# Moving all preparation of the last product's weights to the feed-forward input, and two tiles without a running bank

## The chip, the core and the metric

The kernel runs on one core of a Trainium2 chip. The metric is the device time of one execution in microseconds: 1590.32 us is the median of three runs (1590.27 to 1590.42). Beside those runs one execution was recorded by the hardware profiler; its rows are what this document quotes. The engines of the core are TensorE (PE; its weight loads are PEld), VectorE (DVE), ScalarE (ACT), GpSimd (POOL) and SyncE (SP), which issues nearly all DMA transfers.

## The reference

One encoder layer is applied to two independent sequences of 512 tokens with 1024 channels, each with 256 memory tokens; everything is float32. What matters here:

```
h = rmsnorm(x) @ w_in                      # u, q, k, v, xq and three gates
branches = s5(u), diff_attention(q, k, v), cross_attention(xq, mem)
x = x + (sum of sigmoid(gate_n) * (branch_n @ w_up_n)) @ w_out
gate, up = split(rmsnorm(x) @ w_ffn_in)    # 1024 -> 2 x 2816
x = x + (silu(gate) * up) @ w_ffn_out      # 2816 -> 1024, "the last product"
y = rmsnorm(x)
```

Cross attention has four heads of width 128: per head and sequence, softmax(q k^T) over 256 memory tokens, times the memory values.

## The kernel before

**Number format.** A float32 product is made of three faster ones: each operand is split in a high and a low part (ScalarE casts the high part, VectorE subtracts it from the source to get the low part; `split`, L134 and L135, or with a scale L137 and L138), and TensorE adds high x high, high x low and low x high. A matmul moves 128 x 512 numbers; every matmul is issued from one helper, so all of them carry line 66.

**Planner and orders.** The program is written as a trace, and a planner orders each engine's instructions by simulated times before the kernel runs; on the chip every engine then works through its list in order. Three things bind the planner. `tc.issue_after(x)` puts the instructions of a block behind x on x's engine. `queued()` puts DMA transfers behind the last weight load on SyncE. Where `PE.on` is true, each TensorE instruction is pinned behind all those traced before it. `PE.on` is true in cross attention and differential attention, false in the feed-forward input up to its last tile, and true from that tile (21) on.

**Cross attention** (L567 to L731). 32 steps: four heads, two sequences, four blocks of 128 queries. Step i computes the scores of step i + 2 (three matmuls of 128 x 256, tile `sc`), the softmax on VectorE and ScalarE (`softmax_parts`: maximum, its scale, exponential, reciprocal, then a product, L541 to L550 and L701), transposes step i's probabilities (`tr`, two 128 x 128), splits them (`xpTh`, `xpTl`), and after each fourth step multiplies them with the values (six matmuls into `oo`). Between these parts `fill(n)` lets TensorE do other work from a queue (L684): the query projections of the later heads, two gates, the values and the first queries of differential attention. A unit of that queue is six matmuls of 512 columns (or as many columns in narrower ones). `fill` keeps an account: it adds n, and issues units while the account is over zero. `finish(g)` empties the queue until g is done; it is called before the scores of a new head. What is left at the end of the steps is done in a row (L727).

**The last product's weights.** The last product uses a scheme of seven products in place of eight over quadrants of the operands; for its weights, sums of quarters must be made and split. Of all the pieces (a piece is four 128 x 128 blocks), 28 are prepared ahead (`NPREP`) and kept in DRAM (`wD`): 16 with all seven parts, 12 with four of the seven. `prepare` (L457) is a generator that does half a piece at a time, or a whole small piece: it loads `raw` (two transfers, L443 and L445), splits three quarters into `hl` (L137 on ScalarE, L138 on VectorE) and writes them to `wD` (L472), makes four sums on GpSimd (L452 to L455), and splits and writes the four results. `raw` has four buffers, `hl` has one for three parts and two for four. `half_piece` advances the generator by one. The 16 full pieces are prepared in cross attention, one half at the end of each step, behind the exponential and the product that follows it; the 12 small ones in tiles 4 to 18 of the feed-forward input, one a tile, behind the tile's last tanh on ScalarE, its last sum on VectorE and its last weight sum on GpSimd.

**The feed-forward input** (L1177 to L1231). 22 tiles (KFF) of 128 gate and 128 up channels for both sequences, again with seven products of 12 matmuls each, 84 matmuls a tile. There are six PSUM banks (`mm`) and two more (`tr`). There are two ways through a tile:

- `running` (L1129, tiles 1 to 20): one bank collects four products, A11, S2, S3 and A22, one on top of the other. Between them ScalarE copies the bank's content (`kept_sum`, L1137: tiles p1, u2, u3), and the next product may be added only after that. VectorE makes four sums of other banks and copies (L1112); the bank's last content is read directly by VectorE (L1211).
- `products` and `quadrants` (tiles 0 and 21): each product has its own bank, ScalarE makes one copy (L1119), and VectorE makes seven sums (L1112). In tile 21 the seven products advance together over k, with the seventh in a `tr` bank.

`activate` multiplies with the norm's factors, applies the tanh (L1208) and writes the tile `ac`, which goes to DRAM (`aD`). The up half is multiplied on GpSimd (L1214), except where it lies in the running bank (L1211 on VectorE). `weights4` loads and splits a tile's weights and makes four sums of them on GpSimd (`ws`, L1032 to L1035). Before tile 20's `activate`, the weights of tile 21 are traced. With tile 21 the first operands of the last product are loaded (`act_pair`), summed and split (L980 to L983, `quad_split`). Then the last product begins, with seven banks at once.

Of the kernel before, what the change touches and what calls it, by code (L numbers as in the profile page):

```python
# [28 lines left out]
KFF = FF // P  # L29
# [10 lines left out]
NPREP = (16, 28)  # L40
# [32 lines left out]
def encoder(ctx: ExitStack, tc: tile.TileContext, a, out):  # L73
# [274 lines left out]
    with yielding(last_s):  # L348
        x_norm(0, norm[0], range(5, 8))
        _, bc = factor(ss1, DM)  # L350
# [106 lines left out]
    def prepare(es_, todo_):  # L457
        pq = es_.enter_context(tc.tile_pool(name="pq", bufs=1, side="right", reuse_waits="tile"))
        raws = []

        def load():
            if len(raws) < len(todo_):
                raws.append(pq.tile([P, 4, P], F32, tag="raw", name="raw", bufs=4))
                with queued():
                    raw_in(raws[-1], *todo_[len(raws) - 1][:2])

        def part(n_, j, w_):
            m, p, _ = todo_[n_]
            k = w_.shape[1]
            hl = pq.tile([P, k, 2, P], F32R, tag=f"hl{k}", name="hl", bufs=k // 2)  # L470
            split(hl[:, :, 0], hl[:, :, 1], w_, scale=0.5)
            nc.sync.dma_start(wD[m, p][:, j : j + k], hl.bitcast(F32))  # L472

        for _ in range(3):
            load()
        yield
        for n_, (m, p, k) in enumerate(todo_):
            load()
            if k == 7:
                part(n_, 4, raws[n_][:, 1:4])  # L480
            if k == 7 or n_ == 0:
                raw_sums(raws[n_])
                yield
            part(n_, 0, raws[n_])
            if n_ + 1 < len(todo_) and todo_[n_ + 1][2] == 4:
                raw_sums(raws[n_ + 1])
            yield
# [96 lines left out]
    xa = phase.enter_context(tc.tile_pool(name="xa", bufs=2, reuse_waits="tile"))  # L584
    xcol = phase.enter_context(tc.tile_pool(name="xcol", bufs=2, reuse_waits="tile"))

    pes = ExitStack()
    prep = prepare(pes, pieces[: NPREP[0]])
    next(prep)

    queue = []
    owed = 0

# [93 lines left out]
    for i in range(-AHEAD, len(steps) + 1):  # L689
        if i + AHEAD < len(steps):  # L690
            h, s, lt = steps[i + AHEAD]
            if h and s == lt == 0:
                finish(xq[h])
            ms = slice(s * NMEM, (s + 1) * NMEM)
            qh, ql = (q_[:, lt * P : (lt + 1) * P] for q_ in qs[h, s])
            sc = bank("sc")
            PE.matmul(sc[:, :NMEM], qh, mkh[h][:, ms], start=True, stop=False)
            PE.matmul(sc[:, :NMEM], qh, mkl[h][:, ms], start=False, stop=False)
            PE.matmul(sc[:, :NMEM], ql, mkh[h][:, ms], start=False, stop=True)
            e, r = softmax_parts(xa, xcol, sc[:, :NMEM], NMEM, P ** -0.5, "x", bufs=3)  # L700
            last_e = last_x, V.tensor_scalar_mul(e, e, r)  # L701
            es[i + AHEAD] = e
        fill(9 if i == 0 else 5)
        if 0 <= i < len(steps):
            h, s, lt = steps[i]
            if lt == 0:
                pT[h, s] = tuple(slot("xT", [P, 2, L], F32R, n_) for n_ in ("xpTh", "xpTl"))
            e = es.pop(i)
            tr = aux()
            for j in range(2):  # L710
                PE.transpose(tr[:, j * P : (j + 1) * P], e[:, j * P : (j + 1) * P], ident)
            split(*(p_[:, :, lt * P : (lt + 1) * P] for p_ in pT[h, s]), tr[:, : 2 * P].rearrange("p (j q) -> p j q", j=2))
        fill(5 if i < len(steps) else 15)
        if i > 0 and steps[i - 1][2] == 3:
            h, s, _ = steps[i - 1]
            pTh, pTl = pT.pop((h, s))
            oo = bank("oo")
            hs = slice(h * P, (h + 1) * P)
            for j in range(2):
                PE.matmul(oo, mvh[s][:, j, hs], pTh[:, j, :], start=(j == 0), stop=False)  # L720
                PE.matmul(oo, mvh[s][:, j, hs], pTl[:, j, :], start=False, stop=False)
                PE.matmul(oo, mvl[s][:, j, hs], pTh[:, j, :], start=False, stop=(j == 1))
            osb = xa.tile([P, L], F32, tag="osb", name="xosb", bufs=1)
            S.copy(osb, oo)
            nc.sync.dma_start(bD[2, h, :, s * L : (s + 1) * L], osb)
        half_piece(last_e)
    while queue:  # L727
        fill(6)
    assert next(prep, None) is None
    pes.close()  # L730
    phase.close()  # L731


# [443 lines left out]
    for i in range(KFF):  # L1177
        w = nxt_w or all7(i)
        nxt_w = None
        if i == 4:  # L1180
            prep = prepare(pes, pieces[NPREP[0] : NPREP[1]])
            next(prep)
        elif i == KFF - 3:
            assert next(prep, None) is None
            pes.close()
            open_tags(fes, side="right", tsa=1, tsb=1)
        if i == KFF - 1:
            with tc.issue_after(last_s[1].ins):
                acts = [act_pair(0, "tsa"), act_pair(1, "tsb", V)]
            PE.on = True  # L1190

        if 0 < i < KFF - 1:
            gf0, gf1, up0, up1 = running(w)
        else:
            ps = products(i, w)
            p0 = next(ps)
            if i == 0:
                for s in range(NS):
                    _, bc = rstd(accs[s], DM)
                    S.copy(accs[s], bc)  # L1200
            gf0, gf1, up0, up1 = quadrants(ps, p0)
        ac = ap2.tile([P, NT], F32, tag="ac", name="ac")

        def activate(s, gf, up):
            nonlocal last_t
            cs = slice(s * L, (s + 1) * L)
            V.tensor_tensor(out=gf, in0=gf, in1=accs[s], op=ALU.mult)
            last_t = S.activation(out=ac[:, cs], in_=gf, func=AF.Tanh, scale=0.5)  # L1208
            if s == 0 and 0 < i < KFF - 1:
                u_ = ap2.tile([P, L], F32, tag="up", name="up", bufs=2)  # L1210
                V.tensor_tensor(out=u_, in0=up, in1=accs[s], op=ALU.mult)  # L1211
                up = u_
            else:
                PO.tensor_tensor(out=up, in0=up, in1=accs[s], op=ALU.mult)  # L1214
            V.scalar_tensor_tensor(out=ac[:, cs], in0=ac[:, cs], scalar=1.0, in1=gf, op0=ALU.add, op1=ALU.mult)
            V.tensor_tensor(out=ac[:, cs], in0=ac[:, cs], in1=up, op=ALU.mult)

        if i == KFF - 1:
            with tc.issue_after(last_sum.ins):
                activate(0, gf0, up0)  # L1220
            break
        with ExitStack() as es_:
            if i == KFF - 2:
                nxt_w = all7(i + 1)
                es_.enter_context(tc.issue_after(last_s[1].ins))
            activate(0, gf0, up0)
            activate(1, gf1, up1)
        nc.sync.dma_start(aD[i], ac)
        if 4 <= i < KFF - 3:
            half_piece((last_t, last_sum, last_ws))  # L1230

# [658 lines left out]
```

## Time and profile before

| what | us |
|---|---|
| median of three runs | 1590.32 |
| the profiled execution | 1590.83 |
| its span, first to last instruction | 1589.0 |
| TensorE busy in the span | 1574.8 |
| VectorE, ScalarE, GpSimd busy | 1096.6, 650.4, 477.6 |
| cross attention's steps, about | 386 to 492 |
| feed-forward input, about | 935 to 1357 |
| last product, from | 1357 |

A row of the timeline has the start in us, the duration, the engine, the line, the operation, the tiles written and read, and in brackets the idle time before it and who ended it. A matmul's row lasts longer than the distance to the next, since matmuls overlap; the distance of two starts is what one costs.

### The profile page before, as it was taken

How to read it: one execution, taken by the hardware profiler on the slowest of the kernel's cores; microseconds unless marked ns; L12 is line 12 of the kernel's file. 1: busy time of each engine (PE TensorE's matmuls, PEld its weight loads, DVE VectorE, ACT ScalarE, POOL GpSimd, SP SyncE). 2: the span in 40 equal slices, each digit the busy share in tenths (PEclk: the TensorE clock that was granted, in tenths of full speed). 3: DMA queues.
4: the chain of work that ended last, by engine and by line, in shares of the span. 5: the costliest groups of instructions: out<-in, count | busy, mean ns of one | idle time of the engine just before them, and what ended most of it. 6: DMA issues, size and time to landing. Idle time of an engine off the chain costs nothing. (4 is left out here: it accounts for less than half of the span.)

```text
span 1589.0 us, 21398 instructions
## 1 busy us (share of the span) xinstructions
PE 1574.8 (99%) x7738; PEld 1310.6 (82%) x7738; DVE 1096.6 (69%) x1819; ACT 650.4 (41%) x1155; POOL 477.6 (30%) x414
## 2 busy tenths in 40 slices
PE   9999999999999999999999999999999999999998
PEld 7888888888898779778888888888888887888777
DVE  7978995076774776866545577666666657988864
ACT  6644223275552465563223343333333334223323
POOL 0010000001333320300443354455555342444663
PEclk9999999999999999999999999999999999999999
DMA  9554623675762121135543422333333323885412
GB/s 358 185 167 130 203 93 119 181 273 199 262 226 103 44 97 41 47 127 188 190 146 120 146 83 90 106 120 120 124 131 116 106 80 130 305 318 188 159 61 106
DMA packets 105674, 237.84 MB, mean 150 GB/s; under 512 B 13664, under 2 KB 45408, under 8 KB 105568
## 3 DMA queue, kind: packets, MB, share of 16 engines
q1 hardware_dynamic: 104992, 236.06, 43.8%
q8 instruction: 61, 1.00, 0.3%
q10 hardware_dynamic: 576, 0.41, 0.1%
q14 instruction: 45, 0.37, 0.1%
HBM read 165.16 MB, written 71.27 MB: 149 GB/s over the span
## 5 line engine op out<-in xcount | busy, mean ns | idle before, releaser
L66 PE MATMUL bkmm<-xh,wh 128*128 128x512 f32 x640 | 255.3, 399 | 0.0
L66 PE MATMUL bkmm<-xh,wl 128*128 128x512 f32 x640 | 250.6, 392 | 0.0
L66 PE MATMUL bkmm<-xl,wh 128*128 128x512 f32 x640 | 250.1, 391 | 0.0
L66 PE MATMUL bkmm<-tl,wh 128*128 128x512 f32 (+1 forms) x621 | 241.0, 388 | 0.0
L66 PE MATMUL bkmm<-th,wl 128*128 128x512 f32 (+1 forms) x621 | 240.9, 388 | 0.0
L66 PE MATMUL bkmm<-th,wh 128*128 128x512 f32 (+1 forms) x621 | 238.0, 389 | 2.4 <-ACT u L1137 1.4
L134 ACT CAST wh<-wf 128x1024 fp32r<-128x1024 f32 (+2 forms) x134 | 117.7, 878 | 232.2 <-PE bkmm L66 202.8
L135 DVE TENSOR_TENSOR wl<-wf,wh 128x1024 fp32r<-128x1024 f32 (+2 forms) x134 | 141.9, 1059 | 61.0 <-ACT wh L134 56.1
L66 PE MATMUL bkmm<-th,w 128*128 128x512 f32 x432 | 140.5, 391 | 2.3 <-DVE nsq L1112 1.2
L66 PEld LDWEIGHTS bkmm<-xh,wh 128*128 128x128 f32 x640 | 120.3, 188 | 26.3 <-issue 3.5
L66 PEld LDWEIGHTS bkmm<-xh,wl 128*128 128x128 f32 x640 | 120.2, 188 | 26.3 <-issue 0.4
L66 PEld LDWEIGHTS bkmm<-th,wh 128*128 128x128 f32 x621 | 116.6, 188 | 27.3 <-ACT u L1137 2.2
L66 PEld LDWEIGHTS bkmm<-xl,wh 128*128 128x128 f32 x640 | 120.4, 188 | 22.2
L66 PEld LDWEIGHTS bkmm<-th,wl 128*128 128x128 f32 x621 | 116.5, 188 | 24.3 <-DVE wl L135 0.2
L66 PEld LDWEIGHTS bkmm<-tl,wh 128*128 128x128 f32 x621 | 116.6, 188 | 23.8
L452 POOL TENSOR_TENSOR raw<-raw 128x128 f32<-128x128 f32 x28 | 25.0, 892 | 288.9 <-DVE nb L543 231.8
L66 PEld LDWEIGHTS bkmm<-th,w 128*128 128x128 f32 x432 | 80.9, 188 | 22.4 <-DVE nsq L1112 2.1
L135 DVE TENSOR_TENSOR wl<-ws,wh 128x1024 fp32r<-128x1024 f32 x44 | 57.1, 1297 | 53.9 <-ACT wh L134 53.4
L792 POOL TENSOR_TENSOR mg<-mg,gl 128x1024 f32<-128x1024 f32 x16 | 43.8, 2737 | 136.8 <-DVE gl L788 132.2
L66 PE MATMUL bkmm<-tl,w 128*128 128x512 f32 x216 | 84.1, 389 | 0.0
L66 PE MATMUL bkmm<-yh,wh 128*128 128x512 f32 x192 | 76.2, 397 | 0.0
L66 PE MATMUL bkmm<-yl,wh 128*128 128x512 f32 x192 | 74.8, 390 | 0.0
(666 smaller groups left out, 3397.1 us busy)
## 6 DMA issues: line engine op xcount, KB each, us to landing
wf<-in_w_in SPq DMA_DIRECT2D x40, 512.0 KB, 4.0
wD<-hl SPq DMA_DIRECT2D x28, 512.0 KB, 2.9
w<-wD SPq DMA_DIRECT2D x28, 512.0 KB, 5.0
gD<-gt SPq DMA_DIRECT2D x24, 512.0 KB, 2.9
gl<-gD SPq DMA_DIRECT2D x24, 512.0 KB, 3.3
wf<-in_w_fg SPq DMA_DIRECT2D x22, 512.0 KB, 3.5
wf<-in_w_fu SPq DMA_DIRECT2D x22, 512.0 KB, 3.4
aD<-ac SPq DMA_DIRECT2D x22, 512.0 KB, 2.6
```

What stands on the lines that cost most here:

```text
L66: return self.put(self.eng.matmul(*args, **kw))
L134: h = S.copy(hi, src)
L135: l_ = V.tensor_tensor(out=lo, in0=src, in1=hi.bitcast(F32), op=ALU.subtract)
L452: PO.tensor_tensor(out=a22, in0=a21, in1=a22, op=ALU.add)
L792: PO.tensor_tensor(out=mg[m], in0=mg[m], in1=gt, op=ALU.add)
```

## The change

Three edits. (1) In cross attention no weights of the last product are prepared: the generator isn't made there and no half piece is advanced. Both fills of a step are 3 in place of 5 (the single one of 9 and the last of 15 stay). (2) In the feed-forward input one generator prepares all 28 pieces; it is made at tile 1 in place of 4, and three half pieces are advanced after each tile from 1 to 18, in place of one from 4 to 18. (3) Tile 20 (KFF - 2) goes through `products` and `quadrants` as tiles 0 and 21 do, and both its up halves are multiplied on GpSimd.

```diff
@@ cross attention
-    pes = ExitStack()
-    prep = prepare(pes, pieces[: NPREP[0]])
-    next(prep)
...
-        fill(9 if i == 0 else 5)
+        fill(9 if i == 0 else 3)
...
-        fill(5 if i < len(steps) else 15)
+        fill(3 if i < len(steps) else 15)
...
-        half_piece(last_e)
     while queue:
         fill(6)
-    assert next(prep, None) is None
-    pes.close()
     phase.close()
@@ feed-forward input
-        if i == 4:
-            prep = prepare(pes, pieces[NPREP[0] : NPREP[1]])
+        if i == 1:
+            pes = ExitStack()
+            prep = prepare(pes, pieces[: NPREP[1]])
             next(prep)
...
-        if 0 < i < KFF - 1:
+        if 0 < i < KFF - 2:
             gf0, gf1, up0, up1 = running(w)
...
-            if s == 0 and 0 < i < KFF - 1:
+            if s == 0 and 0 < i < KFF - 2:
...
-        if 4 <= i < KFF - 3:
-            half_piece((last_t, last_sum, last_ws))
+        if 1 <= i < KFF - 3:
+            for _ in range(3):
+                half_piece((last_t, last_sum, last_ws))
```

## The prediction

> **What bounds the kernel now.** First the head of the page, then the longest waits of TensorE.
>
> ```profile
> span 1589.0 us, 21398 instructions
> ...
> PE 1574.8 (99%) x7738; PEld 1310.6 (82%) x7738; DVE 1096.6 (69%) x1819; ACT 650.4 (41%) x1155; POOL 477.6 (30%) x414
> ```
>
> ```profile
> PE bkmm L66 <- ACT u L1137: 1.4, 1, 1.4
> ...
> PE bkmm L66 <- DMA w<-wD: 0.6, 1, 0.6
> ```
>
> TensorE lacks 1589.0 - 1574.8 = 14.2 us of the whole span, and its waits are single ones of 1.4 us and less. The change neither adds nor removes a matmul, so it can win only idle time of TensorE, and it loses only where it makes TensorE wait. So I read the stages that it touches: busy time in stretches (columns: length, PE, PEld, DVE, ACT, POOL, clock, DMA share, GB/s) in cross attention, in the feed-forward input with and without preparation, and at its end.
>
> ```profile
> 386.00:411.00 25.00, 25.00 (x130) 20.77 (x128) 18.83 (x53) 15.02 (x38) 9.22 (x19) 1.00 0.70 247
> ...
> 1088.00:1107.00 19.00, 19.00 (x86) 15.73 (x85) 12.47 (x17) 7.04 (x11) 9.93 (x9) 1.00 0.38 125
> ...
> 1297.00:1316.00 19.00, 19.00 (x86) 15.73 (x85) 11.48 (x16) 6.45 (x10) 7.21 (x5) 1.00 0.24 84
> ...
> 1336.00:1357.00 21.00, 20.08 (x88) 16.17 (x87) 20.39 (x27) 8.15 (x10) 1.83 (x2) 1.00 0.28 90
> 1357.00:1376.00 19.00, 18.43 (x81) 14.94 (x80) 16.75 (x20) 4.88 (x6) 10.24 (x6) 1.00 0.95 358
> ```
>
> TensorE is full, at the full clock (1.00), in cross attention and in every tile of the feed-forward input. Only at the seam of tiles 20 and 21 (1316 to 1357 us) does it miss time, and there VectorE is busy 20.39 of 21 us. The timeline of TensorE at that seam:
>
> ```profile
> 1321.79 0.39 PE L66 MATMUL bkmm<-tl,wh 128*128 128x512 f32 x1
> ...
> 1331.54 0.39 PE L66 MATMUL bkmm<-th,wl 128*128 128x512 f32 x1
> 1333.37 0.50 PE L66 MATMUL bkmm<-th,wh 128*128 128x512 f32 x1 [1.44 <-ACT u L1137]
> ...
> 1339.43 0.39 PE L66 MATMUL bkmm<-th,wl 128*128 128x512 f32 x1
> 1340.74 0.47 PE L66 MATMUL bkmm<-th,wh 128*128 128x512 f32 x1 [0.92 <-DVE up L1211]
> ...
> 1356.57 0.39 PE L66 MATMUL bkmm<-th,w 128*128 128x512 f32 x1
> ```
>
> From 1321.79 to 1331.54 there are 43 steps, so one matmul costs 9.75 / 43 = 0.2267 us at full pace (its 0.39 us overlaps the next). At 1333.37 the gap is 1.83, so 1.60 us is lost: the running bank may not be added to until ScalarE has copied it. At 1340.74 it is 1.31, so 1.08 us is lost: the sixth bank of tile 21 is the running bank, which VectorE (L1211) has not read yet. What ScalarE and VectorE did:
>
> ```profile
> 1331.78 1.04 ACT L134 CAST wh<-ws 128x1024 fp32r<-128x1024 f32 x1 [2.07 <-PE bkmm L66]
> 1332.74 0.58 ACT L1137 COPY u<-bkmm 128x512 f32<-128x512 f32 x1
> ```
>
> ```profile
> 1339.92 0.68 DVE L1211 TENSOR_TENSOR up<-bkmm,acc 128x512 f32<-128x512 f32 x1
> ...
> 1353.44 0.69 DVE L1112 TENSOR_TENSOR u<-bkmm,p 128x512 f32<-128x512 f32 x1 [0.61 <-PE bkmm L66]
> ```
>
> The copy stood behind a weight cast that itself waited. Tile 21 is pinned to program order on TensorE, so nothing could be put into the gap.
>
> **The last two tiles.** Tile 20 takes the path of tile 21: seven banks, one copy (L1119), seven sums (L1112). Matmuls: 84 as before. ScalarE loses two copies of 0.58 us. VectorE has 7 sums for 4 sums and L1211: two more of 0.69, 1.4 us. GpSimd has one more product of L1214, 1.29 us (its row is below). The first wait goes, since no matmul of tile 20 follows a copy: -1.60 us, at worst 0, if a sum late on VectorE holds a bank instead. The second was VectorE's lateness: the last bank of tile 20 is still emptied by a sum among the pair sums and splits that fill 20.39 of 21 us; between 0 and -1.08 I take half, -0.5. What is late next: tile 21 then ends about 2 us sooner, while VectorE has 1.4 us more to do before it empties tile 21's banks, the first at 1353.44 after 0.61 us of idleness; the last product starts at 1356.57 and takes a further bank every 3 x 0.2267 = 0.68 us, as fast as one sum. So of 1.4 - 0.61 = 0.8 us between none and all comes back; I take +0.3. The wait of 0.6 us on w<-wD hangs on a buffer that tile 21 itself frees, and moves along. Sum: -1.60 - 0.5 + 0.3 = -1.8 us.
>
> **Cross attention with a fill of 3.** Units come in sixes, so a step holds 6 filler matmuls instead of 10 on average. The groups of this stage (columns: busy, mean ns, idle before) and one transpose:
>
> ```profile
> L546 ACT ACTIVATE e<-bksc,nb 128x256 f32<-128x256 f32 x32 | 15.2, 475 | 22.4 <-DVE nb L543 22.4
> L135 DVE TENSOR_TENSOR wl<-wf,wh 128x1024 fp32r<-128x1024 f32 x12 | 14.9, 1242 | 3.2 <-ACT wh L134 3.0
> ...
> L541 DVE TENSOR_REDUCE nb<-bksc 128x1 f32<-128x256 f32 x32 | 13.4, 420 | 9.5 <-PE bksc L66 9.0
> L135 DVE TENSOR_TENSOR xpTl<-bktr,xpTh 128x256 fp32r<-128x256 f32 x32 | 13.3, 416 | 1.7 <-ACT xpTh L134 1.7
> L701 DVE TENSOR_SCALAR e<-e,r 128x256 f32<-128x256 f32 x32 | 12.8, 400 | 0.9
> ...
> L546 ACT ACTIVATION_READ_ACCUMULATOR e<-bksc,nb 128x1 f32 x32 | 6.2, 195 | 0.0
> ...
> L135 DVE TENSOR_TENSOR ql<-bkmm,qh 128x512 fp32r<-128x512 f32 x8 | 5.5, 682 | 0.0
> ...
> L550 DVE RECIPROCAL r<-sm 128x1 f32<-128x1 f32 x32 | 5.2, 161 | 12.5 <-ACT e L546 12.1
> ...
> L543 DVE TENSOR_SCALAR nb<-nb 128x1 f32<-128x1 f32 x32 | 4.7, 148 | 0.5
> ```
>
> ```profile
> 428.75 0.48 PE L66 MATMUL bkmm<-xh,wh 128*128 128x512 f32 x1
> ...
> 429.07 0.39 PE L66 MATMUL bkmm<-xl,wh 128*128 128x512 f32 x1
> ...
> 430.22 0.28 PE L66 MATMUL bksc<-mkvh,qh 128*128 128x256 f32 x1
> ```
>
> A step of TensorE is then 6 x 0.227 = 1.36 us of filler, three scores of half width (0.34), two transposes (0.11, an estimate by a quarter of the width each), 0.09 for the slow matmul after them (429.07 - 428.75 - 0.227), and a quarter of six output matmuls (0.34): 2.24 us, against 3.15. VectorE needs 0.420 + 0.148 + 0.161 + 0.400 + 0.416 = 1.55, and per 48 filler matmuls (8 steps) one wl and two ql, (1.242 + 1.364) / 8 = 0.33: 1.87 us, 83% of 2.24. The latency from scores to transposes is 0.420 + 0.148 + 0.475 + 0.195 + 0.161 + 0.400 = 1.80 us; with a wl, a ql and an xpTl in front of it 4.14. Three fillers, two transposes and two scores give it 4.08 + 0.40 + 0.68 = 5.2 us. So it stays hidden. The filler is not lost: the queue holds 8 x 48 = 384; before, 35 steps took 364, now 228, plus some 42 that finish() forces ahead of the third head; some 114 x 0.227 = 26 us run densely after the steps. Cost 0. Bounds: the five matmuls from 429.07 to 430.22 took 0.230 each, 0.003 over the dense pace, so the 136 - 42 = 94 moved out could win 0.3 us (136 = 364 - 228); and +3.2 us (a rival below).
>
> **The preparation.** Each tile from 1 on gets three half pieces; 16 x 2 + 12 = 44, so tiles 1 to 15. Now the tile raw and hl alone, in cross attention and in the feed-forward input (columns: DVE, ACT, POOL), GpSimd's waits, and SyncE's part:
>
> ```profile
> 386.00:486.00 100.00, 19.29 (x31) 17.99 (x31) 31.28 (x63) 1.00 0.66 232
> 1012.00:1240.00 228.00, 7.46 (x11) 6.78 (x11) 34.73 (x44) 1.00 0.34 116
> ```
>
> ```profile
> L1216 DVE TENSOR_TENSOR ac<-ac,up 128x512 f32<-128x512 f32 x24 | 16.6, 692 | 17.2 <-POOL up L1214 16.8
> ...
> L452 POOL TENSOR_TENSOR raw<-raw 128x128 f32<-128x128 f32 x11 | 15.9, 1445 | 0.0
> ...
> L1214 POOL TENSOR_TENSOR up<-up,acc 128x512 f32<-128x512 f32 x12 | 15.5, 1290 | 38.0 <-DVE up L1112 38.0
> ```
>
> ```profile
> L443 SPq DMA_DIRECT2D raw<-in_w_fo x28: 372/426/1127, 350.6 to 1183.3; - x28
> L445 SPq DMA_DIRECT2D raw<-in_w_fo x28: 427/713/785, 351.1 to 1183.8; - x28
> ...
> L472 SPq DMA_DIRECT2D wD<-hl x44: 319/326/775, 384.6 to 1258.6; - x44
> ```
>
> A half piece is 19.29 / 31 = 0.62 us of VectorE and 17.99 / 31 = 0.58 of ScalarE; a piece's four sums are 34.73 / 11 = 3.16 us of GpSimd here (four times 31.28 / 63, 2.0, in cross attention). Three half pieces: VectorE 11.48 + 1.87 = 13.4 of 19, ScalarE 6.45 + 1.74 = 8.2, GpSimd 7.21 + 1.5 x 3.16 = 11.9, and in the last four such tiles 7.21 + 3 x 3.16 = 16.7. SyncE gets up to three pieces a tile, 3 x (0.426 + 0.713 + 0.326) = 4.4 us of issue. In bytes, three small pieces (128 x 512 in, 128 x 1024 out, 0.79 MB each by their shapes) put 2.36 MB / 19 us = 124 GB/s on top of 84, under the 358 of 1357 to 1376. All fits into 19 us: cost 0, hidden behind a full TensorE. If the cover is thin, it is GpSimd's up product (L1214) that waits behind raw sums, VectorE that waits for it (already 16.8 us in 12 tiles, 1.4 each), and the bank sums queued behind it; that is a rival. Below 0 it cannot go: TensorE has nothing to win there, nor in cross attention from the work taken out.
>
> The Trainium skill (SBUF — State Buffer, Who interferes with whom) says that a VectorE instruction with two SBUF inputs and a GpSimd one that reads SBUF lock each other out for their whole length. The 1445 ns of L452 beside a split, against 31.28 / 63 = 0.50 us in cross attention, agree. By it 64 moved raw sums could each hold VectorE for half a microsecond, 32 us over 15 tiles, 2.1 a tile: 15.5 of 19, still under the tile, so the sum would stay and the slower rival gains weight.
>
> **The rivals.** (1) Nothing is won: VectorE, full from 1336 to 1357, holds a bank of tile 20 or 21 for what the copies held before. 1590.3 us. Against it: a sum is 0.69 and a product of twelve matmuls 2.7 us. (2) Slower: in the feed-forward input four raw sums (3.16 us) stand ahead of the up product, and VectorE's in-order queue waits with the bank sums behind it. It decides once the lateness exceeds a product's 2.72 us: 0.44 us for each of 15 tiles, 6.6 us: 1588.5 + 6.6 = 1595.1. For it: GpSimd at 16.7 of 19. Against: VectorE's 5.6 idle us a tile. (3) The short step: VectorE's 1.87 us and its wait for the exponential, 12.1 / 32 = 0.38, are 2.25 against 2.24; if other waits add 0.1 us a step, 32 x 0.1 = 3.2: 1591.7. (4) More is won: both waits whole, the wait on w<-wD and the dense filler: 1.60 + 1.08 + 0.6 + 0.3 = 3.6, 1586.7; for it speaks that each wait is there now, against it VectorE's 20.39 of 21 us.
>
> **How the numbers follow.** The profiled execution took 1590.83 us (span 1589.0 and 1.8 around it), 0.5 above the median of 1590.32. 1590.83 - 1.8 = 1589.0 in its terms, 1588.5 for the median. Chances: forecast 0.50, (1) 0.20, (2) 0.13, (3) 0.10, (4) 0.07. The forecast's own range is 1587.2 to 1590.0; the range that holds all but part of (2) and (4) is 1586.8 to 1593.8. What a measurement can tell from no change is 0.2%, 3.2 us: faster than 1587.1 is (4) and a little of the forecast, 0.09; slower than 1593.5 is (2), with a tail of (3) less its milder part, 0.13; the same 0.78.
>
> **What will show it.** Right: no wait of TensorE on ACT u L1137 at the end of the feed-forward input, the wait on DVE under 1 us, cross attention's steps 2.3 us apart with PE at 25.00 of 25.00, every tile 19.0 us. Wrong: tiles 1 to 15 longer than 19.05 us with TensorE waiting for ACT u or a bank (2), waits on e or bktr between the steps (3), a new wait on DVE sums at 1335 to 1360 as long as the old ones (1).

## The result, and the profile after

The changed kernel takes 1627.61 us (median of four runs, 1625.71 to 1629.77) against 1590.30 (1590.19 to 1590.42): 1.0235 times as long, 95% interval 1.0217 to 1.0253, or 37 us more. The profiled execution took 1626.21 us. In code that stands behind the edits its line numbers are lower by 7 to 9 (L1137 is now L1128, L1208 is L1200, L1214 is L1206, L1017 is L1008). First the head of its page and the longest waits of TensorE (line waited for, us in total, times, longest):

```profile
span 1624.4 us, 21353 instructions
...
PE 1588.2 (98%) x7738; PEld 1310.3 (81%) x7738; DVE 1114.2 (69%) x1821; ACT 649.2 (40%) x1153; POOL 486.7 (30%) x415
```

```profile
PE bkmm L66 <- ACT u L1128: 15.6, 10, 2.0
PE bkmm L66 <- DVE wl L135: 7.0, 12, 1.0
```

The work is the same, and the shares of the span are nearly the same. But TensorE is idle for 1624.4 - 1588.2 = 36.2 us instead of 14.2, and its "busy" time rose by 13.4 with the same 7738 matmuls: the row of a matmul that starts after a wait lasts 0.50 us in place of 0.39, and some run at half the clock (last section). Busy time in stretches tells where (columns as in the prediction): cross attention, nine tiles with three half pieces each, and a stretch without any preparation.

```profile
386.00:411.00 25.00, 25.00 (x138) 21.00 (x137) 17.35 (x63) 13.29 (x41) 0.00 (x0) 1.00 0.13 44
1026.10:1221.00 194.90, 178.95 (x750) 140.83 (x749) 131.43 (x163) 69.86 (x107) 109.04 (x113) 0.98 0.48 161
1264.00:1285.00 21.00, 21.00 (x93) 17.19 (x92) 16.24 (x22) 7.84 (x12) 8.45 (x7) 1.00 0.45 164
```

The same view of the kernel before, over eleven tiles:

```profile
1055.20:1263.90 208.70, 208.70 (x922) 172.80 (x921) 137.72 (x177) 77.10 (x110) 103.14 (x91) 1.00 0.35 120
```

A tile has 84 matmuls. Before, it took 84 x 208.70 / 922 = 19.0 us; now it takes 84 x 194.90 / 750 = 21.8. That is 2.8 us in a tile that carries preparation. Tiles 1 to 15 carry it, and 13 such tiles would already make the whole loss (13 x 2.8 = 36.4). Cross attention is as full as it was, and behind the last preparation (1264) TensorE is full again. No engine got full: per tile VectorE is busy 131.43 x 84 / 750 = 14.7 of 21.8 us, ScalarE 7.8, GpSimd 12.2. What is late can be followed in the timelines of one tile, from one reload of the up half's weights (`wf<-in_w_fu`) to the next. The rows stand by engine: SyncE, GpSimd, ScalarE, VectorE, TensorE; x2 is two instructions in one row.

```profile
1090.77 0.52 SPq L1008 DMA_DIRECT2D wf<-in_w_fu  x1
...
1113.16 0.33 SPq L1008 DMA_DIRECT2D wf<-in_w_fu  x1
...
1096.62 1.29 POOL L1023 TENSOR_TENSOR ws<-wf 128x512 f32<-128x512 f32 x1 [8.10 <-DMA wf<-in_w_fu]
...
1105.86 0.46 POOL L452 TENSOR_TENSOR raw<-raw 128x128 f32<-128x128 f32 x1 [3.62 <-DVE hl L138]
...
1108.33 0.46 POOL L455 TENSOR_TENSOR raw<-raw 128x128 f32<-128x128 f32 x1
...
1097.87 0.64 ACT L1200 ACTIVATE ac<-gf 128x512 f32<-128x512 f32 x1 [6.57 <-DMA aD<-ac]
1100.89 1.05 ACT L134 CAST wh<-ws 128x1024 fp32r<-128x1024 f32 x1 [2.39 <-POOL ws L1024]
1103.95 0.63 ACT L1200 ACTIVATE ac<-gf 128x512 f32<-128x512 f32 x1 [2.00 <-DVE gf L1199]
1104.49 0.51 ACT L137 ACTIVATE hl<-raw 128x384 fp32r<-128x384 f32 x1
1105.84 0.58 ACT L1128 COPY u<-bkmm 128x512 f32<-128x512 f32 x1
...
1108.82 1.05 ACT L137 ACTIVATE hl<-raw 128x512 fp32r<-128x512 f32 x2 [1.92 <-POOL raw L455]
1109.78 1.56 ACT L134 CAST wh<-wf 128x512 fp32r<-128x512 f32 x2
...
1101.98 1.33 DVE L135 TENSOR_TENSOR wl<-ws,wh 128x1024 fp32r<-128x1024 f32 x1 [1.68 <-ACT wh L134]
1103.24 0.68 DVE L1199 TENSOR_TENSOR gf<-gf,acc 128x512 f32<-128x512 f32 x1
...
1105.23 0.55 DVE L138 SCALAR_TENSOR_TENSOR hl<-raw,hl 128x384 fp32r<-128x384 f32 x1
...
1109.49 1.57 DVE L138 SCALAR_TENSOR_TENSOR hl<-raw,hl 128x512 fp32r<-128x512 f32 x2 [1.49 <-ACT hl L137]
...
1112.18 0.95 DVE L135 TENSOR_TENSOR wl<-wf,wh 128x512 fp32r<-128x512 f32 x1
...
1106.47 0.49 PE L66 MATMUL bkmm<-th,wh 128*128 128x512 f32 x1 [1.21 <-ACT u L1128]
```

Read in order of time this is a ring. The reload (1090.77) lands and GpSimd makes the sums (1096.62). ScalarE casts them (1100.89), VectorE takes the low part (1101.98) and then, in its order, the gate's product (1103.24); then come the tanh (1103.95), one half piece's cast (1104.49), a weight cast, and only then the copy (1105.84) for which TensorE stands until 1106.47. In the same tile VectorE takes the half piece's low part (1105.23); GpSimd waits for that before it makes the raw sums (1105.86 to 1108.79); ScalarE's next cast of `hl` waits for the sums (1108.82), and the A22 cast stands behind it (1109.78). VectorE's low part of A22 (1112.18) frees the weight buffer, and SyncE reloads (1113.16). The ring took 22.4 us, and none of its steps waited for TensorE. In the kernel before, the same ring took 18.97 us:

```profile
1093.05 0.33 SPq L1017 DMA_DIRECT2D wf<-in_w_fu  x1
...
1112.02 0.33 SPq L1017 DMA_DIRECT2D wf<-in_w_fu  x1
...
1096.61 1.28 POOL L1032 TENSOR_TENSOR ws<-wf 128x512 f32<-128x512 f32 x1 [5.51 <-DMA wf<-in_w_fu]
...
1108.74 0.62 ACT L134 CAST wh<-wf 128x512 fp32r<-128x512 f32 x1 [0.95 <-ACT p L1137]
```

There the A22 cast started 15.7 us after the reload (1108.74 - 1093.05), and no cast of `hl` that had waited for raw sums stood right in front of it; now it starts 19.0 us after (1109.78 - 1090.77). Of these 3.3 us, 2.3 are lost before any engine works: the first weight sum starts 5.85 us after the reload in place of 3.56 (1096.62 - 1090.77 and 1096.61 - 1093.05), because the reload lands later. This tile is the extreme one. In the mean of the stretches above (reloads from 1026.06 to 1221.05 and from 1055.21 to 1263.91), the round grew from 19.0 to 21.7 us. Of these 2.7 us, 1.6 lie between the reload and the first weight sum (5.15 in place of 3.57), 0.5 between that and the end of A22's low part, and 0.6 between that end and the next reload, which still stands in SyncE's queue.

### The profile page after: what moved, and what is told of

Same layout as the page of the kernel before. It is cut to its first block, busy times and chain, and to the rows that moved or that the text cites. A ratio compares the mean times of both kernels' runs of the same rounds, so it can differ in the third digit from the quotient of the medians.

```text
span 1624.4 us, 21353 instructions
## 1 busy us (share of the span) xinstructions
PE 1588.2 (98%) x7738; PEld 1310.3 (81%) x7738; DVE 1114.2 (69%) x1821; ACT 649.2 (40%) x1153; POOL 486.7 (30%) x415
## 5 line engine op out<-in xcount | busy, mean ns | idle before, releaser
L66 PE MATMUL bkmm<-th,wh 128*128 128x512 f32 (+1 forms) x621 | 243.2, 394 | 17.9 <-ACT u L1128 15.6
L135 DVE TENSOR_TENSOR wl<-wf,wh 128x1024 fp32r<-128x1024 f32 (+2 forms) x134 | 150.0, 1119 | 77.6 <-ACT wh L134 73.2
L744 POOL TENSOR_TENSOR t<-t,rs 128x512 f32<-128x512 f32 x16 | 26.6, 1662 | 462.5 <-DVE t L743 462.5
L1200 ACT ACTIVATE ac<-gf 128x512 f32<-128x512 f32 x44 | 27.8, 632 | 145.7 <-DMA aD<-ac 86.7
L1207 DVE SCALAR_TENSOR_TENSOR ac<-ac,gf 128x512 f32<-128x512 f32 x44 | 37.3, 847 | 60.7 <-ACT ac L1200 60.7
```

The costliest lines, as they stand in the source:

```text
L66: return self.put(self.eng.matmul(*args, **kw))
L135: l_ = V.tensor_tensor(out=lo, in0=src, in1=hi.bitcast(F32), op=ALU.subtract)
L744: PO.tensor_tensor(out=t2, in0=t2, in1=rope[1], op=ALU.mult)
```

## The experiments

**Which of the three edits.** First the kernel before with the two other edits, and the changed kernel without them.

```diff
 e1_no_move: kernel before, with
-        fill(9 if i == 0 else 5)
+        fill(9 if i == 0 else 3)
...
-        if 0 < i < KFF - 1:
+        if 0 < i < KFF - 2:
 e2_move_only: changed kernel, with both of these undone
```

> The kernel before with the fill of 3 and tile 20 without the running bank, but the preparation where it was. Theory T1: the loss comes from the move of the preparation alone, through a chain of the engines other than TensorE that must close once a tile (reload of the up weights' buffer, sums on GpSimd, casts on ScalarE, low parts on VectorE). Then every tile of the feed-forward input is back at 19.0 us and the total is within 3 us of 1590.3. Theory T2: the loss comes from the fill or from tile 20. Then some 35 us stay.

> The changed kernel with the fills of 5 and with the running bank in tile 20, so the move of the preparation alone. T1: tiles 2 to 15 take 21 to 22 us, total 1620 to 1630. T2: total near 1590.

The first took 1591.81 us, a ratio of 1.0009 [0.9999, 1.0018]; the second 1625.64, 1.0219 [1.0199, 1.0240]. The move alone is the loss. The first differs from the kernel before by no more than can be measured. Its trace shows a small price, though: with preparation still beside cross attention, a fill of 3 makes TensorE's transposes there wait for VectorE's maxima, two times and 1.4 us in all; in the changed kernel, where preparation is gone from there, no such wait is left.

**Tile 20 alone.**

```diff
 e4_tile20: kernel before, with
-        if 0 < i < KFF - 1:
+        if 0 < i < KFF - 2:
...
-            if s == 0 and 0 < i < KFF - 1:
+            if s == 0 and 0 < i < KFF - 2:
```

> The kernel before with the third edit alone: tile 20 without the running bank, the fill of 5 and the preparation where they were. The seam of tiles 20 and 21 lost 1.60 and 1.08 us in the profile before and 1.2 us in e1. If the step of the prediction on tile 20 holds, 1.0 to 2.0 us are won: 1588.3 to 1589.3, ratio 0.9987 to 0.9994. If the waits only change their names: 1590.3.

1589.35 against 1590.48 us, 0.9994 [0.9985, 1.0003]. The interval reaches from a gain of 2.4 us to a loss of 0.5, so a gain is not shown. In its trace the two waits at the seam are gone, and one of 1.2 us for tile 21's low weight parts on VectorE is left.

**Engines or transfers.** Two kernels prepare everything in cross attention and only imitate the preparation in the feed-forward input: one makes the casts, low parts and sums of three half pieces a tile on data that stays there, without their transfers; the other makes the transfers alone. Cramming all preparation into cross attention costs both a wait of 12 us behind it, so only their tiles are read. In what was expected of them, T1a is the theory that casts of the preparation, waiting for raw sums ahead of the A22 cast, close the ring late, T1b that the transfers make the reload late, and T3 that GpSimd is too busy; the expectation of e3, further down, introduces them.

```diff
 z_comp: changed kernel, with
-            prep = prepare(pes, pieces[: NPREP[1]])
+            prep = imitate(pes, pieces[: NPREP[1]], True, False)   # compute, no transfers
...
 z_dma:
+            prep = imitate(pes, pieces[: NPREP[1]], False, True)   # transfers, no compute
```

> All 28 pieces are prepared beside cross attention (two half pieces a step at its end), and the feed-forward input gets only an imitation of the half pieces: the same casts, low parts and raw sums, three half pieces a tile, on four raw tiles loaded once; their results are not stored. So the engines' work of the preparation is there and its transfers are not. T1a: tiles of 20.5 us or more. T1b: tiles of 19.0 to 19.5 us. T3: tiles of 20.5 or more.

> The counterpart of z_comp: all 28 pieces prepared beside cross attention, and in the feed-forward input an imitation with the transfers alone: the raw loads and writes of the same sizes, three half pieces a tile, each write released by a copy of one column on VectorE; no casts, low parts or raw sums. T1a: tiles of 19.0 to 19.4 us. T1b: tiles of 20.5 us or more. From z_comp (20.7) and the changed kernel (21.5) some 0.8 us a tile could be the transfers'.

Stretches of seven tiles with full pieces, of the first and of the second:

```profile
1021.30:1166.00 144.70, 137.34 (x592) 111.46 (x591) 100.87 (x127) 54.97 (x85) 78.55 (x79) 0.99 0.22 77
```

```profile
1017.50:1149.70 132.20, 132.20 (x585) 109.49 (x584) 95.30 (x127) 44.71 (x63) 54.01 (x35) 1.00 0.51 176
```

With the engines' work alone a tile takes 84 x 144.70 / 592 = 20.5 us; with the transfers alone 84 x 132.20 / 585 = 19.0, and TensorE is full at 176 GB/s. So transfers by themselves cost nothing, and the engines' part makes 1.5 of the 2.8 us (1630.0 and 1610.0 us in all). The rest appears only with both. One thing that then differs is that reloads which stand right behind the preparation's transfers land later. In the two stretches above the first weight sum starts 3.5 us after the reload, as in the kernel before; in the changed kernel 5.15. From issue to landing of the up half's weights over the whole kernel (minimum, median, maximum), before and after:

```profile
DMA to landing us min/median/max: 3.3/3.4/4.7
```

```profile
DMA to landing us min/median/max: 3.4/4.7/5.8
```

**The running bank.** TensorE waits longest for the copies of the running bank. Is the bank the cause?

```diff
 e7_no_running: changed kernel, with
-        if 0 < i < KFF - 2:
+        if False:
...
-            if s == 0 and 0 < i < KFF - 2:
+            if False:
```

> The changed kernel with no running bank in any tile, so that no matmul waits for a copy of ScalarE. T2b (the loss is ScalarE's copies of the running bank, 15.6 us of waits in the changed kernel): tiles near 19.5 us, total 1595 to 1605. T1: the chain is not of the copies, TensorE waits for weights in their place, tiles of 21 us, total 1615 to 1630.

1621.76 us, 1.0197 [1.0178, 1.0215], 6 us less than the changed kernel. Without copies the longest wait has another name, and is no shorter:

```profile
PE bkmm L66 <- DVE wl L135: 23.4, 21, 3.5
```

So the copy was mostly the place where lateness showed.

**The order of the same work.** In e3 the second half of a full piece is prepared after the first half of the next, so no cast waits for raw sums of the same tile. In e6 the three half pieces come half a tile later, behind the cast and low part of the next tile's A22. In e8 both. Work and transfers are the same in all.

```diff
 e3_sums_early, in prepare: part(n - 1, 0) is traced behind raw_sums(n), not behind raw_sums(n - 1)
 e6_behind_a22: changed kernel, with
-                half_piece((last_t, last_sum, last_ws))    # behind the tile
+                half_piece((*last_a22, last_ws))           # behind the next tile's A22 split
 e8_behind_and_early: both
```

> The changed kernel with the same half pieces in another order: a full piece's second half follows the first half of the next piece, so that its cast on ScalarE does not wait for the four raw sums that GpSimd has just begun. T1a (within T1, ScalarE's wait for those sums, 2.0 us ahead of the cast of the next up weights, is what closes the chain late): tiles fall by about 2 us, to 19.0 to 19.8, total 1592 to 1602. T1b (the reload is late because SyncE and the DMA queues carry the preparation's transfers): tiles stay above 21, total above 1618. T3 (GpSimd is too busy, the rival of the prediction): no change, since the same sums are made.

> The changed kernel with the same half pieces, three a tile, but one half tile later and, on ScalarE and VectorE, behind the cast and the low part of the next tile's A22 weights, the step that frees the buffer of the up weights. T1a (casts of the preparation ahead of that cast close the chain late): tiles of 19.0 to 20.0 us, total 1592 to 1605. T1b (transfers) and T3 (GpSimd's load): tiles above 21 us as in the changed kernel, total 1620 or more.

> The changed kernel with both mends together: half pieces behind the A22 weights (e6, 1603.8) and sums a half piece earlier (e3, 1609.9). T1: both shorten the same chain, so tiles of 19.0 to 19.6 and a total of 1592 to 1600, but not under the kernel before, since TensorE's 19.04 us a tile stay. If the remaining 13 us of e6 are the transfers' or the end's, 1601 to 1605.

They took 1609.92 us (1.0120 [1.0105, 1.0135]), 1603.82 (1.0083 [1.0070, 1.0097]) and 1610.49 (1.0127 [1.0111, 1.0144]): e3 between its two expectations, e6 inside that of T1a, e8 above both. Stretches with full pieces of the first and of the second:

```profile
1023.30:1161.00 137.70, 134.36 (x588) 109.68 (x587) 96.60 (x126) 54.13 (x84) 83.70 (x80) 1.00 0.48 170
```

```profile
1020.90:1159.40 138.50, 136.26 (x591) 109.86 (x590) 103.03 (x127) 54.88 (x85) 78.21 (x79) 1.00 0.48 168
```

Both tiles are 19.7 us (84 x 137.70 / 588, 84 x 138.50 / 591), with engines about as busy per tile as in the changed kernel. Order alone took back 18 and 24 of 37 us. But an order of the work is also an order of its transfers, and the rows say that this is where most of it came from. The landing of the reload in e6, to be compared with the two views above:

```profile
DMA to landing us min/median/max: 3.3/3.6/4.6
```

Here is the round from reload to reload, in the mean of each run's stretch with full pieces (in the two imitations their likeness, in the kernel before one small piece a tile; us, from the rows of SyncE, GpSimd and VectorE):

| run | round | reload to first weight sum | to the end of A22's low part | to the next reload |
|---|---|---|---|---|
| before | 18.97 | 3.57 | 15.37 | 0.03 |
| engines alone (z_comp) | 20.67 | 3.50 | 17.14 | 0.03 |
| transfers alone (z_dma) | 18.89 | 3.55 | 15.31 | 0.03 |
| changed | 21.67 | 5.15 | 15.87 | 0.65 |
| e3 | 19.68 | 3.92 | 15.73 | 0.03 |
| e6 | 19.78 | 3.68 | 16.07 | 0.03 |
| e8 | 20.08 | 4.24 | 15.82 | 0.03 |

From the changed kernel to e6 the round falls by 1.9 us: 1.5 because the reload lands sooner, 0.6 because it no longer stands in SyncE's queue once its buffer is free. The engines' part of the round isn't shorter. So the expectation of e6 was met in its time, but the reason it gave, the casts ahead of the A22 cast, is not what the rows show. In z_comp the reload lands on time and the round is still 1.7 us longer than before, so the engines' part isn't free either; no run separates the two in the changed kernel. e8 is no better than e3, which my theory had not expected; its reload lands later than in e6, and why is open.

**Is there slack in the ring before?** Two needless ScalarE copies of 0.6 us, once inside the ring ahead of a weight cast, once where ScalarE was idle.

```diff
 e9_copies_in_chain: kernel before, in weights4
...
+            for _ in range(2):
+                extra = S.copy(scr, s12[:, :L])
+        with tc.issue_after(extra.ins):
             sp(aps, s34, "s", "S3", "S4")
 e10_copies_beside: the same copies behind the cast of S1 and S2, and no issue_after(extra)
```

> The kernel before with two needless copies of 128x512 a tile on ScalarE (about 0.6 us each, their results unused), placed behind the tile's last tanh and ahead of the cast of the next tile's S3 and S4 weights. In the profile before, the reloads of the up weights are 18.97 us apart (1055.2 to 1263.9, 11 tiles) and no link of the chain from reload to reload waits for TensorE, whose own tile is 19.04 us. T1, sharpened: the chain had no slack even before, so what is put into one of its links is paid in every tile: 18 tiles times about 1.0 us, total 1605 to 1614, though ScalarE stays under 45% busy. If the chain had slack (2 us or more), total 1590 to 1593.

> The same two copies a tile, placed behind the cast of the S1 and S2 weights, where ScalarE sat idle for 2.8 us before the tanh. T1, sharpened: the same work beside the chain costs nothing, total 1590 to 1593. If it is ScalarE's load that counts, the same loss as in e9.

1594.13 us (1.0020 [1.0009, 1.0030]) and 1590.36 (0.9999 [0.9989, 1.0010]). The first was expected to lose 15 us and more. It lost 4, at the first tiles; in the fifteen tiles behind them TensorE is full, at 84 x 285.60 / 1262 = 19.0 us:

```profile
1042.50:1328.10 285.60, 285.60 (x1262) 236.49 (x1261) 194.16 (x238) 119.41 (x178) 135.73 (x115) 1.00 0.33 113
```

The ring of the kernel before can therefore take 1.2 us more, or the planner's new order around the copies made room. "No slack at all" was wrong. The trace of the changed kernel agrees: behind the last preparation, where the weights catch up with TensorE, three reloads go out at 1282.02, 1299.39 and 1316.85, 17.4 us apart. Without half pieces the ring needs no more than that.

**Cutting the ring at a buffer.** If the reload closes the ring, a third weight buffer should cut it. If the tile `ac` does (the tanh above waited 6.57 us for its transfer), halves of it with transfers of their own should.

```diff
 e11_third_buffer: changed kernel (e12_before_third: kernel before; e13_behind_and_third: e6), with
-        a1, a2 = (wp.tile([P, DM], F32, tag="wf", name="wf") for _ in range(2))
+        a1, a2 = (
+            aps.tile([P, DM], F32, tag="wf3", name="wf", bufs=1) if n % 3 == 2 else wp.tile([P, DM], F32, tag="wf", name="wf")
+            for n in (2 * i, 2 * i + 1)
+        )
 e14_ac_halves: changed kernel (e15_halves_third: e11; e16_before_halves: kernel before), with
-        ac = ap2.tile([P, NT], F32, tag="ac", name="ac")
+        ach = [ap2.tile([P, L], F32, tag=f"ac{s}", name="ac") for s in range(NS)]
...
+            if i < KFF - 1:
+                nc.sync.dma_start(aD[i][:, s * L : (s + 1) * L], ac)
...
-        nc.sync.dma_start(aD[i], ac)
```

> The changed kernel with one edit: the feed-forward input's weight loads take turns over three buffers in place of two (the third in a pool of its own), so a tile's reload of w_fu goes into the buffer that the tile before's gate weights left, and no longer waits for the cast and low part of the same tile's A22 weights. All work, its order of tracing and all transfers stay. Theory (a chain closed once a tile through that buffer): the loop is cut, TensorE sets the pace again, tiles with full pieces fall from 21.6 to between 19.0 and 19.8 us, and the kernel to 1591 to 1601 us, without a change in the order of preparation. Rival (it is not the loop: the engines' waits within a tile, casts behind raw sums or low parts behind each other, last over 21 us wherever the weights come from): tiles stay at 21 us or more and the time over 1615. Between 1601 and 1615: both have a part.

> The kernel before with the third buffer alone, as the control of the run with the third buffer in the changed kernel. If the loop isn't what sets the tile before (TensorE is: 19.04 us), nothing changes: 1589.8 to 1591.0. If the tile's loop set the pace before as well, it would win up to the few tenths that a tile misses: 1587 to 1589.

> The changed kernel with both: three buffers for the feed-forward input's weights, and the three half pieces half a tile later, behind the cast and low part of the next tile's A22 weights. Closed chain: with the loop cut, the order matters little, and what the late order still lost (19.8 us a tile, 1603.8) goes as well: 1590 to 1597, tiles 19.0 to 19.4. Rival (what was left there is contention of VectorE and GpSimd or slower transfers): 1600 to 1606, tiles 19.7 to 19.9.

> The changed kernel with one edit: the tile ac (128 x 1024, one buffer) is two tiles of 128 x 512, each written to DRAM by its own transfer when its half is done, so the first tanh of a tile waits for the first half's transfer alone. Same memory, one DMA more a tile. In the changed kernel that tanh stands idle 6.57 us until the transfer of ac has landed, and with it ScalarE and the sums behind it on VectorE. Theory A (the period is closed through ac: tanh, hl, casts, low parts, last product of ac, transfer, tanh): tiles fall from 21.6 us by 1 to 2.4 us, the kernel to 1592 to 1610. Theory B (it is closed through the reload of w_fu alone): the tanh comes earlier but the casts of the weight sums still wait for w_fu: tiles stay over 21 us, 1618 to 1627.

> The changed kernel with ac in halves and with three buffers for the feed-forward input's weights. Both loops are longer by some microseconds of slack. If the two loops (through ac, and through the weight buffers) close side by side and each alone keeps the period, only this run falls clearly: 1592 to 1606, while the one with the third buffer alone gave 1618.4. If it is the order within a tile (VectorE's and ScalarE's in-order waits for the raw sums, low parts slowed beside GpSimd): over 1612.

> The kernel before with ac in halves alone, as the control. There the first tanh waits 0.80 us for ac, and TensorE for nothing: 1589.5 to 1591.5 by both theories.

| run | us | ratio to before |
|---|---|---|
| changed, third buffer (e11) | 1618.44 | 1.0177 [1.0162, 1.0192] |
| before, third buffer (e12) | 1598.71 | 1.0051 [1.0034, 1.0067] |
| later order, third buffer (e13) | 1615.61 | 1.0160 [1.0145, 1.0175] |
| changed, `ac` in halves (e14) | 1628.31 | 1.0245 [1.0226, 1.0263] |
| changed, both (e15) | 1632.47 | 1.0265 [1.0249, 1.0281] |
| before, `ac` in halves (e16) | 1590.59 | 1.0002 [0.9993, 1.0012] |

No buffer opened the ring, so "closed through this one buffer" fell. By their times e11, e14 and e15 fit what their expectations set against it: in e11 and e15 the order of waits within a tile, in e14 the reload (Theory B, though 1 us above its range). The traces add that the ring closed elsewhere or in the same place. In e11 the reload went into a buffer that another low part on VectorE had to free, at once behind it:

```profile
1093.14 1.22 DVE L135 TENSOR_TENSOR wl<-wf,wh 128x1024 fp32r<-128x1024 f32 x1
...
1094.38 0.33 SPq L1011 DMA_DIRECT2D wf<-in_w_fu  x1
```

In e14 the tanh still waited 7.03 us for the transfer of `ac`, and the reload went out 0.2 us after A22's low part had ended (1109.18 + 0.95), as soon as SyncE had issued the raw loads and writes that stood in front of it; so two closures end together there:

```profile
1109.18 0.95 DVE L135 TENSOR_TENSOR wl<-wf,wh 128x512 fp32r<-128x512 f32 x1
...
1110.35 0.41 SPq L1008 DMA_DIRECT2D wf<-in_w_fu  x1
```

The control e12 was expected to change nothing and lost 8 us, so the third buffer is not free, and e11 is no clean test of the ring: what the buffer opens, its price can take back. It moves the weight sums beside VectorE's low parts, and these then take longer. In e12 and, for the same instruction, in the kernel before:

```profile
1091.07 1.78 DVE L138 SCALAR_TENSOR_TENSOR hl<-raw,hl 128x512 fp32r<-128x512 f32 x1
```

```profile
1106.04 0.68 DVE L138 SCALAR_TENSOR_TENSOR hl<-raw,hl 128x512 fp32r<-128x512 f32 x1
```

The Trainium skill (SBUF — State Buffer, Who interferes with whom), which the prediction cites, says that such a pair locks each other out; the trace agrees (0.68 becomes 1.78 us). Run e13 was expected to end at 1606 us at most; there the reload lands later still, 5.7 us after its issue in the median against 3.6 in e6.

**The dose.** The last run moves less: four full pieces stay in cross attention, and tiles 1 to 18 get two units each, first two halves of a full piece, later two small pieces.

```diff
 e18_two_units: kernel before, with
-    prep = prepare(pes, pieces[: NPREP[0]])
+    prep = prepare(pes, pieces[:4])
...
-        half_piece(last_e)
+        if i <= 8:
+            half_piece(last_e)
...
-        if i == 4:
-            prep = prepare(pes, pieces[NPREP[0] : NPREP[1]])
+        if i == 1:
+            pes = ExitStack()
+            prep = prepare(pes, pieces[4 : NPREP[1]])
...
-        if 4 <= i < KFF - 3:
-            half_piece((last_t, last_sum, last_ws))
+        if 1 <= i < KFF - 3:
+            for _ in range(2):
+                half_piece((last_t, last_sum, last_ws))
```

> The kernel before with part of the move: 4 of the 16 full pieces stay in cross attention (its first steps, fills as before), 12 go to the feed-forward input with the small ones, and each of the tiles 1 to 18 gets two half pieces (or two small pieces) in place of three. Running bank and fills as before. Theory (several loops of about the same length share the links low part, raw sums, cast, low part in the in-order queues; a tile is longer only by what the longest loop exceeds 19.04 us, and two half pieces in one tile are one whole piece with only one cast that waits for fresh raw sums): tiles 19.0 to 19.8 us, the kernel 1590 to 1603. Rival (each half piece costs its share by contention): before, one small piece a tile costs nothing, three cost 2.5 us a tile; two cost about half, 1.2 us in each of 18 tiles: 1609 to 1615.

1618.20 us, 1.0172 [1.0155, 1.0188], above both expectations. Its stretches with one full piece a tile, and with two small ones:

```profile
1024.00:1191.70 167.70, 154.68 (x673) 125.50 (x673) 108.46 (x137) 58.44 (x89) 78.83 (x76) 1.00 0.39 132
1214.10:1312.00 97.90, 94.21 (x411) 76.25 (x410) 67.69 (x86) 36.23 (x54) 60.50 (x61) 1.00 0.47 160
```

A tile with one full piece takes 84 x 167.70 / 673 = 20.9 us, though GpSimd is busy less than half of it (78.83 of 167.70); one with two small pieces takes 84 x 97.90 / 411 = 20.0, with more work a tile on VectorE and GpSimd (13.8 and 12.4 us against 13.5 and 9.8). So it is not the amount of the engines' work. A full piece has what a small one lacks: a cast that waits for raw sums, which wait for the low part of its first half. Its rows on SyncE, GpSimd, ScalarE and VectorE:

```profile
1086.62 0.37 SPq L1018 DMA_DIRECT2D wf<-in_w_fu  x1
...
1080.05 0.45 POOL L452 TENSOR_TENSOR raw<-raw 128x128 f32<-128x128 f32 x1 [4.34 <-DVE hl L138]
...
1083.01 0.63 ACT L137 ACTIVATE hl<-raw 128x512 fp32r<-128x512 f32 x1 [1.92 <-POOL raw L455]
...
1083.68 1.11 DVE L138 SCALAR_TENSOR_TENSOR hl<-raw,hl 128x512 fp32r<-128x512 f32 x1 [1.49 <-ACT hl L137]
...
1085.91 0.68 DVE L135 TENSOR_TENSOR wl<-wf,wh 128x512 fp32r<-128x512 f32 x1
```

VectorE's low part, four raw sums, a cast, another low part (ends 1084.79), two operations of the tile, A22's low part (ends 1086.59), and only then, at 1086.62, the reload of the tile's weights. This is one difference. The other is again the transfers: the raw loads of the full piece were issued right in front of the reload (the second at 1085.67), and the first weight sum starts 4.4 us after it in the mean of this stretch, against 3.6 with two small pieces. Which of the two lengthens the tile more was not tested.

**What stands and what is open.** Shown: the move alone loses the 37 us, in the tiles that carry preparation; transfers alone cost nothing there, and the engines' work alone 1.5 of 2.8 us a tile; with the same work, its order (that of its transfers with it) changes the loss by 24 us; and one full piece a tile costs more than two small ones. Read from rows, not isolated: that the tile's period is a ring over SyncE, GpSimd, ScalarE and VectorE, in which several closures (weight buffer, SyncE's queue, `ac`) are about equally long, so that opening one leaves the next; and that reloads which stand right behind the preparation's transfers land later. A run that moves only these transfers out of the reload's way is missing. Open: why 13.5 us remain in e6, why e8 and e13 give gains back, and how much of the third buffer's loss is contention. No version tried beats the kernel before by more than can be measured; e4 is the nearest.

## Why the prediction was wrong

**The step that failed** is "All fits into 19 us: cost 0, hidden behind a full TensorE". Instead a tile became 21.8 us long and the kernel lost 37 us. The sums behind the step nearly held: 13.4, 8.2 and 11.9 us of VectorE, ScalarE and GpSimd a tile were predicted, 14.7, 7.8 and 12.2 measured. What did not follow is that work which fits is hidden. Busy sums bound a tile only if each engine can run ahead. Here the engines work in a fixed order and hand a tile's weights round once; the question was how long that round trip becomes when each half piece adds a cast, a low part, four sums and a place in SyncE's queue to it. The trace of before shows that ring, with a reload every 18.97 us. This is TensorE's own pace, so the distance doesn't tell the slack: e9 shows room for 1.2 us, and the 17.4 us behind the preparation show 1.6 where no half piece is prepared. The 3.16 us of raw sums and the casts behind them had to be asked for their place on that ring, not for their share of 19 us. The same holds for SyncE: its 4.4 us of issue and the 124 GB/s were summed and fit, as z_dma shows, but the step did not ask what stands ahead of the reload. In the changed kernel the reload's landing and queue make 2.2 of the 2.7 us by which the round grew. How much of the loss each link would cost by itself stays open.

**"Below 0 it cannot go"** held, but it was the only bound that the step gave. What the move costs if the cover is missing stood only in rival (2), with 6.6 us, and the range ended at 1593.8.

**Rival (2)** had the place and the sign: tiles 1 to 15, with TensorE waiting. Its mechanism, GpSimd's up product behind raw sums, is not in the ring of the rows above (between 1000 and 1245 us no product of VectorE waits for it), and its 0.44 us a tile were 2.8. The sign that the prediction named for it, tiles over 19.05 us with TensorE waiting for ACT u, is what came.

**Tile 20** was predicted at -1.8 us; alone it measured -1.1, which is not clear of zero. Both waits on the running bank went. What came next was not VectorE's sums, as the step had it, but tile 21's weights. In the changed kernel the seam has three waits, 0.84 + 1.03 + 0.53 = 2.4 us:

```profile
1371.26 0.50 PE L66 MATMUL bkmm<-th,wl 128*128 128x512 f32 x1 [0.84 <-DVE wl L135]
1373.48 0.50 PE L66 MATMUL bkmm<-th,wh 128*128 128x512 f32 x1 [1.03 <-ACT wh L134]
1374.74 0.50 PE L66 MATMUL bkmm<-th,wl 128*128 128x512 f32 x1 [0.53 <-DVE wl L135]
```

**Cross attention** was right: 25.00 of 25.00 with 138 matmuls, cost 0. The waits that rival (3) feared appear only where preparation stays beside it (e1).

## What to carry to other kernels

A full TensorE hides work only as long as the longest ring of hand-overs among the other engines closes within TensorE's time for a tile; so follow that ring in the trace, from one reload of a buffer to the next, before adding to any engine on it. Where TensorE is full, the distance of two reloads is TensorE's; the ring's own length shows where TensorE isn't the limit, or when a known delay is put in, as in e9. Count added work as latency along the ring (what it waits for, and what stands behind it in each in-order queue, SyncE's too), not as a share of busy time. A buffer more helps only if no other closure of the ring is nearly as long; putting the added work, and with it its transfers, behind the ring's own links took back more than buffers did.

## What the hardware did that was not expected

After some waits of about 2 us in sum the granted clock halved. Two stretches of the changed kernel, and TensorE around the first:

```profile
1173.00:1176.00 3.00, 3.00 (x9) 2.33 (x8) 1.58 (x3) 1.14 (x2) 2.84 (x5) 0.50 0.69 240
1213.00:1217.00 4.00, 4.00 (x11) 3.12 (x12) 3.94 (x6) 1.58 (x3) 0.58 (x1) 0.59 0.84 286
```

```profile
1171.76 0.50 PE L66 MATMUL bkmm<-th,wh 128*128 128x512 f32 x1 [1.99 <-ACT u L1128]
...
1173.26 0.63 PE L66 MATMUL bkmm<-th,wl 128*128 128x512 f32 x1
1173.68 0.63 PE L66 MATMUL bkmm<-th,wh 128*128 128x512 f32 x1
```

For some 3.4 us the matmuls start 0.42 us apart instead of 0.23, about 1.6 us lost on top of the wait, twice in this run. Other waits of nearly that length were not followed by it (1.84 us, ended at 1259.36). The Trainium skill (TensorE: Matmul & The Clock Gate, Part 1: The HAM clock gate) puts the fall to half clock after an idle window of about 3.4 us; here the fall followed 1.99 us of idle time, and in the second case 1.06 and 0.96 us close together, so by this trace shorter gaps can precede it.
